# Raw DeltaNet tiles of the drain's sums in buffers of their own, inverses and turned outputs some steps later, in a hybrid mLSTM and DeltaNet layer

## The chip, the cores and the metric

The kernel runs on one core of a Trainium2 chip. The metric is the device time of one execution in microseconds; the median of several runs is given. Engine names are those of the profile: PE multiplies matrices, DVE, ACT and POOL do vector, activation and general work, SP issues transfers.

## What is computed

One layer of a decoder block on 512 tokens of width 2048, all in float32. A normalised input u is projected once; the parts feed an mLSTM with 8 heads and a gated DeltaNet with 16 heads; each branch's output goes through its half of the output projection, and the two results are gated and added to x, with a norm at the end.

```python
u = _rmsnorm(h, norm_w)
proj = jnp.matmul(u, w_in)                       # 2048 x 20528
h_a = _mlstm_chunkwise(q, k, v, i_pre, logf)     # 8 heads, chunks of 64
h_b = _gated_delta_chunkwise(dq, dk_, dv_, beta, g)
y_a = jnp.matmul(h_a, w_out[:ML_WIDTH])
y_b = jnp.matmul(h_b, w_out[ML_WIDTH:])
return jax.nn.sigmoid(gate_a) * y_a + jax.nn.sigmoid(gate_b) * y_b
```

In the DeltaNet each chunk solves a unit lower triangular system (the inverse below) before a chain over the chunks:

```python
a_mat = jnp.where(strict, bc[..., :, None] * kk * decay_mat, 0.0)
lhs = a_mat + jnp.eye(CHUNK)
sol = lax.linalg.triangular_solve(lhs, rhs, lower=True, unit_diagonal=True)
```

## The kernel before, in words

**Products.** Each float32 product is done as three matmuls: weights and activations are split into a high and a low part, and high·high, high·low and low·high are summed. A weight comes from memory into one of four buffers (`wr`, pool `wp`), ACT makes its high part (L135, `wh`) and DVE its low part (L138, `wl`). A list `plan` says in which order the weights are loaded (L176), and `prepare` keeps loads 4 and splits 3 weights ahead of PE.

**Stages by time in the trace.** Up to 100 us the input is prepared. To about 1060 the wide projections run as products of sums (seven matmuls in place of eight). From 1070 to 1846 the mixers run: eight units, each with two DeltaNet heads and, in four of them, one mLSTM head, whose projections (`proj_cm`, L250 to L265, bank `pj`) are interleaved with the mixers' small matmuls. From 1846 the output projection runs. Its mLSTM half is three wide blocks of 16 weights (`wide_block`, L1284 to L1286 in `products`): block 0 from 1846, block 1 from 1904, block 2 from 1966. Beside blocks 0 and 1 the last unit's inverse, back substitution and chain drain. From 2029 to 2187 the first part of the DeltaNet half runs as seven products (weights L505, their sums L528 and L535), and a last block ends at 2248.

**What sets the order.** PE's order is the program's. Side work is written as generators: `start(gen, wait)` puts one on a list, and `tick()`, called every six matmuls or so, lets each that is due issue its next piece; what it yields is the number of steps until the next. A step is some 1.4 us of matmuls. The instructions of the other engines are placed by a scheduler with priorities (`urgent`), and `behind(engine)` places one after the engine's newest weight split (for SP, its newest weight load). Each engine, and each engine's queue of transfers, then runs its instructions in that order.

**The parts that the change touches.**

- `turn` (L792) turns a finished output tile by a transpose on DVE (L796) into `to`, and `travel` (L799) issues four transfers of it on ACT's queue (L806) to h_d (DeltaNet) or hm_d (mLSTM) in memory, three steps after. For other tiles the same code issues on SP's queue, to `td` and back (L811).
- `dn_front_k` (L814) sends the DeltaNet's k products to memory and back in another layout, `ls` (L870), and inverts 128 systems of 32 by 31 pairs of DVE instructions (L881, L883). The result goes out and back (L895, L896) and is transposed into `tn` (L899), which the substitution reads (copies `ta` L951, `tb` L968; `vt` L972; matmuls `pw` L998). In the chain `r` (L993) and `st` (L1009) are DVE's, read by PE at L998 and L990.
- The conv rows: ACT copies a projection's bank out (`yp`, L770) and so frees the bank.
- `h_sums` (L1220) prepares the seven products. For each of eight pairs of DeltaNet heads it loads both heads' tiles of h_d (`hs`, `load_tile` L1177), makes three sums (L1237 to L1239) and a fourth in place (L1240) on DVE, stores that one to he_d from ACT's queue, and splits the sums (L1180, L1181). Its raw tiles come from `wp`, tag `wr`: the ring of four in which the weights lie. `load_h2` then loads the same h_d and he_d again as `hr` for the full products.
- `close` opens the pools for it: `sa2` when the first scratch pool (B) is no longer used, `sb2` when the second (A, `wk`) is free too. The last pair waits for `sb2`.
- The gates `tgy` of the wide blocks are loaded (L1299) into `wk` for block 0, tags `dm` and `rb`; block 1's into `wp`, tag `tg`.

Of the kernel before, what the change touches and what calls it, by code (L numbers as in the profile page):

```python
# [8 lines left out]
F32 = mybir.dt.float32  # L9
F32R = mybir.dt.float32r  # L10
AF = mybir.ActivationFunctionType
ALU = mybir.AluOpType
# [3 lines left out]
P = 128  # L16
S = 512
# [5 lines left out]
NO = 512  # L23
NRAW, NSPL = 4, 4
# [5 lines left out]
HP = S // 2  # L30
KH = KT // 2
# [15 lines left out]
UNITS = [(p, p + 1 if 2 * QKFIRST - 2 < p < 7 else None) for p in range(8)]  # L47
# [8 lines left out]
def hybrid_body(  # L56
# [16 lines left out]
    nc = tc.nc  # L73
    ctx.enter_context(tc.manual_schedule(engines={mybir.EngineType.PE}))
    V, A, G, T = nc.vector, nc.scalar, nc.gpsimd, nc.tensor
# [3 lines left out]
    wp = ctx.enter_context(tc.tile_pool(name="wp", bufs=4))  # L79
    dr = ctx.enter_context(tc.tile_pool(name="dr", bufs=1, space=DRAM))  # L80
    rows_d = dr.tile([32, S], F32, tag="rows", name="rows_d")
    h_d = dr.tile([KT, 16, BS, 4, BS], F32, tag="hd", name="h_d")
# [57 lines left out]
    def behind(eng):  # L140

        return tc.issue_after(newest[eng])
# [74 lines left out]
    def start(gen, wait=0, by=None):  # L217
        active.append([gen, clock["t"] + wait, held["by"] if by is None else by])
# [570 lines left out]
            with urgent():  # L789
                A.activation(jk, pk[:, c, :], AF.Square, accum_out=dst[:, c:c + 1])  # L790

    def turn(src, dst, out=False):  # L792


        o = dst if dst is not src and len(dst.shape) == 3 else wk.tile([P, NC, P], F32, tag="to", name="to", bufs=2)
        V.transpose(o if len(src.shape) == 3 else o.rearrange("p n c -> p (n c)"), src)  # L796
        start(travel(o, dst, out), 3 if out else 2)

    def travel(o, dst, out):  # L799

        d = dst if len(dst.shape) == 4 else dr.tile([16, BS, 4, BS], F32, tag="td", name="td", bufs=8)
        ov = o.rearrange("p n (j c) -> p (n j) c", c=BS)
        q = nc.scalar if out else nc.sync
        with behind("A") if out else urgent(2):
            for a in range(4):
                q.dma_start(d[:, :, a, :].rearrange("m r c -> r m c"), ov[a * BS:(a + 1) * BS])  # L806
        if d is dst:
            return
        yield 4
        with behind("A") if out else urgent(2):  # L810
            q.dma_start(dst, d.rearrange("(n j) r a c -> (j r) n (a c)", n=NC))  # L811
        yield 1

    def dn_front_k(hs, kq, u):  # L814
# [57 lines left out]
        G.memset(xi, 0.0)  # L872
        for q in range(4):
            G.memset(xi.rearrange("p m t -> p (m t)")[q * NSYS:(q + 1) * NSYS, q:(BS // 4) * BS:BS + 4], 1.0)
        yield 7
        for i in range(BS - 1):
            n, m = BS - 1 - i, i // 4 + 1
            tmp = wkb.tile([P, 80], F32, tag="tmp", name="tmp")
# [14 lines left out]
        with urgent():  # L893
            for q in range(4):
                nc.sync.dma_start(xd[:, :, :, q, :].rearrange("g b m t -> (g b) m t"), xi[q * NSYS:(q + 1) * NSYS])  # L895
            nc.sync.dma_start(tt, xd.rearrange("g b m q t -> (b m q) g t"))  # L896
        yield 14
        with urgent(), behind("V"):
            V.transpose(tn.rearrange("p g m -> p (g m)"), tt.rearrange("p g t -> p (g t)"))  # L899
        u.update(tn=tn, tt=tt)  # L900
# [75 lines left out]
    def dn_chain(j, hs, kq, u):  # L976
        h = hs[j]
        aq, qt, ke, ge = u["aq"][j], u["qt"][j], u["ke"][j], u["dm"][j][2]
        vn = u["vs"][j]

        po = pso.tile([P, NC, P], F32, tag="o", name="po")
        ssq = wk.tile([P, NC], F32, tag="ssq", name="ssq")
        st = None
        for c in range(NC):
            tsl = slice(c * P, (c + 1) * P)
            if st is None:
                r = vn[:, c, :]
            else:
                pr = psw.tile([P, P], F32, tag="wk", name="pr")
                T.matmul(pr, kq[j][:, 0, tsl], st, start=True, stop=True)  # L990
                r = wk.tile([P, P], F32, tag="r", name="r")
                with urgent():
                    V.scalar_tensor_tensor(out=r, in0=pr, scalar=negeg[:, c, h:h + 1], in1=vn[:, c, :],  # L993
                                           op0=ALU.mult, op1=ALU.add)
                T.matmul(po[:, c, :], qt[:, c, :], st, start=True, stop=False)
                yield 2
            pw = psw.tile([P, P], F32, tag="wk", name="pw")
            T.matmul(pw, tb[:, j * NC + c, :], r, start=True, stop=True)  # L998
            w = wk.tile([P, P], F32, tag="w", name="w")
            with urgent():  # L1000
                A.copy(w, pw)
            yield 2
            if c < NC - 1:
                pst = psw.tile([P, P], F32, tag="wk", name="pst")
                T.matmul(pst, ke[:, c, :], w, start=True, stop=True)
                sn = wk.tile([P, P], F32, tag="st", name="st", bufs=4)
                with urgent():
                    if st is None:
                        V.tensor_copy(sn, pst)  # L1009
                    else:  # L1010
                        V.scalar_tensor_tensor(out=sn, in0=st, scalar=ge[:, c:c + 1], in1=pst,
                                               op0=ALU.mult, op1=ALU.add)
            T.matmul(po[:, c, :], aq[:, c, 1, :], w, start=(st is None), stop=True)
            if c == 1:
                g = wk.tile([P, NC, P], F32, tag="g", name="gz", bufs=2)
                nc.sync.dma_start(g, gz_d[:, :, h * P:(h + 1) * P].rearrange("c p n -> p c n"))
            if c < NC - 1:
                st = sn
                yield 2

        jk = wk.tile([P, P], F32, tag="jk", name="jk", bufs=1)
        for c in range(NC):
            with urgent():
                A.activation(jk, po[:, c, :], AF.Square, accum_out=ssq[:, c:c + 1])
        with urgent():
            V.scalar_tensor_tensor(out=ssq, in0=ssq, scalar=1.0 / P, in1=u["qe"][:, j, :], op0=ALU.mult, op1=ALU.add)
        rsd = wk.tile([P, NC], F32, tag="rsd", name="rsd")
        G.tensor_tensor(out=rsd, in0=ssq, in1=mhalf, op=ALU.pow)
        G.tensor_tensor(out=g, in0=g, in1=bc(rsd, P), op=ALU.mult)
        yield 2  # L1030
        with urgent():
            V.tensor_tensor(out=g, in0=po, in1=g, op=ALU.mult)
        turn(g, h_d[h], True)

    def dn_unit(p, mh):
        hs = (2 * p, 2 * p + 1)
# [139 lines left out]
    def load_tile(dst, src):  # L1176
        nc.sync.dma_start(dst.rearrange("p (n t) -> p n t", n=NC), src.rearrange("(n j) r a c -> (j r) n (a c)", n=NC))  # L1177

    def split_scaled(hi, lo, src, w):
        A.activation(hi, src, AF.Copy, scale=w)  # L1180
        V.scalar_tensor_tensor(out=lo, in0=src, scalar=w, in1=hi.bitcast(F32), op0=ALU.mult, op1=ALU.subtract)  # L1181
# [35 lines left out]
    late = {}  # L1217
    he_d = dr.tile([KH, P, S], F32, tag="hed", name="he_d")

    def h_sums():  # L1220

        for i in range(KH):
            if i == KH - 1:
                while "sb" not in late:
                    yield 1
                yield 2
            su = (late["sa"] if i < KH - 1 else late["sb"]).tile([P, 2, 3, HP], F32R, tag=f"su{i}", name="tu", bufs=1)
            late["su"].append(su)
            raw = []
            for n in range(2):  # L1230
                raw.append(wp.tile([P, S], F32, tag="wr", name="hs", bufs=NRAW))
                load_tile(raw[n], h_d[2 * i + n])
            yield 3
            a11, a21, a12, a22 = (raw[n][:, m * HP:(m + 1) * HP] for n in range(2) for m in range(2))
            sf = late["sa"].tile([P, 3, HP], F32, tag="sf", name="hsum", bufs=2)
            with behind("V"):
                V.tensor_tensor(out=sf[:, 0], in0=a21, in1=a22, op=ALU.add)  # L1237
                V.tensor_tensor(out=sf[:, 1], in0=sf[:, 0], in1=a11, op=ALU.subtract)
                V.tensor_tensor(out=sf[:, 2], in0=a11, in1=a21, op=ALU.subtract)  # L1239
                V.tensor_tensor(out=a21, in0=a12, in1=sf[:, 1], op=ALU.subtract)  # L1240
            yield 1
            with behind("A"):
                nc.scalar.dma_start(he_d[i], raw[0])
            with behind("A"), behind("V"):
                split_scaled(su[:, 0], su[:, 1], sf, normc[:, 32:33])
            yield 3

    def load_h2():

# [21 lines left out]
    def close():  # L1271
        if "su" not in late and not using("B"):
            wkbs.close()
            sa = h2s.enter_context(tc.tile_pool(name="sa2", bufs=1, side="right"))
            late["sa"], late["su"] = sa, []
            start(h_sums(), 1)
        if "sb" not in late and "su" in late and not using("AB"):
            wks.close()
            sb = late["sb"] = h1s.enter_context(tc.tile_pool(name="sb2", bufs=1))
            late["X"] = sb.tile([P, 2, 2, NO], F32, tag="X", name="X2")  # L1280

    def products(ps, kt, c, hi, lo, ks):
        tsl = slice(c * P, (c + 1) * P)
# [7 lines left out]
    def wide_block(nb, pools, place, then=()):  # L1291
# [37 lines left out]
        for c in range(NC):  # L1329
# [6 lines left out]
            else:  # L1336
                start(put_last(), 1)

    DRAIN = (lambda c: wk.tile([P, NO], F32, tag=("dm", "rb")[c // 2], name="tgy", bufs=2 + c // 2),
             lambda c: wp.tile([P, NO], F32, tag="tg", name="tgy", bufs=3))  # L1340
    for b in range(YDRAIN):
        wide_block(b, ((psj, "pj"), (psw, "wk"), (psj, "pj"), (psj, "pj")), DRAIN[b])
# [281 lines left out]
```

## Time and profile before

| | |
|---|---|
| median of 3 runs | 2246.78 us (2246.72 to 2247.63) |
| profiled execution | 2249.86 us |
| its span, first to last instruction | 2247.8 us |
| PE busy | 2162.3 us (96%) |
| mean granted clock of TensorE | 0.990 |

The profiled execution is 3.1 us above the median; its span is 2.1 us below its own time. In the waits and groups a row reads: engine, output tile and line, what it waited for, then total us, times and the longest. In a timeline a row has start and duration in us, and in brackets how long the engine was idle before it and what released it. The granted clock is 1.00 at full speed and 0.50 at half.

### The profile page before, as it was taken

The numbers are of one execution on the slowest core, as the hardware profiler recorded it, in microseconds if no ns is written. First come the engines' busy times: TensorE is split into PE (matmuls) and PEld (weight loads), VectorE is DVE, ScalarE is ACT, GpSimd is POOL, SyncE is SP. The second block draws the span as 40 slices with busy tenths as digits, with TensorE's granted clock in tenths as the row PEclk, the third lists the DMA queues.
The fourth block names the chain that finished last, engine by engine and source line by source line (L and its number), as shares of the span: only waits on it lengthen the run. The fifth ranks groups of instructions, "written<-read, shape, count | busy, mean of one in ns | idle before, by whom it ended". The sixth has DMA issues, their size and how long they took to land. (4 is left out here: it accounts for less than half of the span.)

```text
span 2247.8 us, 31587 instructions
## 1 busy us (share of the span) xinstructions
PE 2162.3 (96%) x10592; PEld 1770.9 (79%) x10592; DVE 1671.8 (74%) x2907; ACT 995.1 (44%) x1890; POOL 280.7 (12%) x356
## 2 busy tenths in 40 slices
PE   7999999999999999999999999999999989879997
PEld 5878778888778888888878877888888877757775
DVE  5787788778877777876678877676767676557775
ACT  5444444445444443444444534444444443334344
POOL 0320000000000000000222422222222211100101
PEclk9999999999999999999999999999999999989999
DMA  5456666667666775776676866767665666595896
GB/s 156 128 171 198 198 195 214 206 191 234 203 214 223 230 233 179 229 253 193 171 187 164 198 150 147 174 167 183 168 162 145 169 170 176 149 271 172 242 327 213
DMA packets 534821, 435.81 MB, mean 194 GB/s; under 512 B 241921, under 2 KB 393698, under 8 KB 534530
## 3 DMA queue, kind: packets, MB, share of 16 engines
q1 hardware_dynamic: 425058, 357.68, 55.7%
q10 hardware_dynamic: 105568, 68.77, 9.7%
q0 software_dynamic: 4032, 7.34, 2.2%
q8 instruction: 83, 1.36, 0.3%
q14 instruction: 80, 0.66, 0.1%
HBM read 342.37 MB, written 95.49 MB: 195 GB/s over the span
## 5 line engine op out<-in xcount | busy, mean ns | idle before, releaser
L135 ACT CAST wh<-wr 128x512 fp32r<-128x512 f32 (+1 forms) x538 | 379.5, 707 | 477.3 <-PE pj L262 221.8
L138 DVE TENSOR_TENSOR wl<-wr,wh 128x512 fp32r<-128x512 f32 (+1 forms) x538 | 449.3, 838 | 168.3 <-ACT wh L135 159.5
L261 PE MATMUL pj<-uh,wh 128*128 128x512 f32 x1024 | 429.0, 419 | 3.1 <-ACT yp L770 3.1
L263 PE MATMUL pj<-uh,wl 128*128 128x512 f32 x1024 | 401.9, 393 | 0.0
L262 PE MATMUL pj<-ul,wh 128*128 128x512 f32 x1024 | 401.2, 392 | 0.0
L576 PE MATMUL ps<-wl,uh 128*128 128x512 f32 x704 | 277.3, 394 | 6.1 <-DVE wl L138 5.8
L575 PE MATMUL ps<-wh,uh 128*128 128x512 f32 x704 | 275.8, 392 | 3.7 <-DVE X L617 3.0
L577 PE MATMUL ps<-wh,ul 128*128 128x512 f32 x704 | 274.4, 390 | 0.0
L135 ACT CAST wh<-ts 128x512 fp32r<-128x512 f32 x224 | 138.1, 617 | 255.0 <-DVE ts L535 196.3
L135 ACT CAST wh<-t 128x1024 fp32r<-128x1024 f32 x112 | 117.8, 1052 | 258.4 <-PE ps L577 136.7
L263 PEld LDWEIGHTS pj<-uh,wl 128*128 128x128 f32 x1024 | 192.8, 188 | 42.6
L576 PE MATMUL ps<-wl,suh 128*128 128x512 f32 x576 | 224.3, 389 | 1.7 <-DVE wl L138 1.7
L575 PE MATMUL ps<-wh,suh 128*128 128x512 f32 x576 | 224.4, 390 | 0.8 <-ACT qk L353 0.4
L261 PEld LDWEIGHTS pj<-uh,wh 128*128 128x128 f32 x1024 | 193.8, 189 | 38.9 <-ACT yp L770 3.9
L577 PE MATMUL ps<-wh,sul 128*128 128x512 f32 x576 | 224.1, 389 | 0.0
L262 PEld LDWEIGHTS pj<-ul,wh 128*128 128x128 f32 x1024 | 193.9, 189 | 32.9
L138 DVE TENSOR_TENSOR wl<-ts,wh 128x512 fp32r<-128x512 f32 x224 | 153.8, 690 | 38.8 <-ACT wh L135 38.8
L138 DVE TENSOR_TENSOR wl<-t,wh 128x1024 fp32r<-128x1024 f32 x112 | 137.2, 1225 | 53.4 <-ACT wh L135 52.9
L576 PEld LDWEIGHTS ps<-wl,uh 128*128 128x128 f32 x704 | 132.1, 188 | 43.1 <-DVE wl L138 17.3
L575 PEld LDWEIGHTS ps<-wh,uh 128*128 128x128 f32 x704 | 132.1, 188 | 37.7 <-DVE X L617 10.2
L577 PEld LDWEIGHTS ps<-wh,ul 128*128 128x128 f32 x704 | 132.2, 188 | 26.6
L535 DVE TENSOR_TENSOR ts<-wr 128x512 f32<-128x512 f32 x112 | 77.3, 690 | 98.7 <-DMA wr<-t_d 74.4
(302 smaller groups left out, 3481.3 us busy)
## 6 DMA issues: line engine op xcount, KB each, us to landing
wr<-in_w_in_dram SPq DMA_DIRECT2D x704, 256.0 KB, 3.7
wr<-in_w_out_dram SPq DMA_DIRECT2D x138, 256.0 KB, 4.6
t_d<-ts ACTq DMA_DIRECT2D x96, 256.0 KB, 4.1
wr<-t_d SPq DMA_DIRECT2D x96, 256.0 KB, 4.0
wr<-in_w_in_dram SPq DMA_DIRECT2D x64, 128.0 KB, 3.4
xt<-in_x_dram SPq DMA_DIRECT2D x8, 512.0 KB, 7.2
tg_d<-X ACTq DMA_DIRECT2D x16, 256.0 KB, 6.1
tg_d<-to ACTq DMA_DIRECT2D x16, 256.0 KB, 5.5
```

Source lines behind the costliest of these rows:

```text
L135: newest["A"] = A.copy(hi, src).ins
L138: newest["V"] = V.tensor_tensor(out=lo, in0=src, in1=hi.bitcast(F32), op=ALU.subtract).ins
L261: T.matmul(ps[j], hi[:, k, wsl], uh[:, kt, :], start=(kt == 0), stop=False)
L262: T.matmul(ps[j], hi[:, k, wsl], ul[:, kt, :], start=False, stop=False)
L263: T.matmul(ps[j], lo[:, k, wsl], uh[:, kt, :], start=False, stop=(kt == KT - 1))
L535: V.tensor_tensor(out=ts[:, 0, :], in0=r[:, 0, :], in1=r[:, 2, :], op=ALU.subtract)
L575: T.matmul(ps[t], ah, hi, start=(g == "A" and i == 0), stop=False, skip_group_check=True)
L576: T.matmul(ps[t], ah, lo, start=False, stop=False, skip_group_check=True)
L577: T.matmul(ps[t], al, hi, start=False, stop=(i == KH - 1), skip_group_check=True)
```

## The change

1. Turned outputs (h_d, hm_d) are issued 5 steps after their transpose instead of 3, but for the last unit's two DeltaNet heads, which keep 3.
2. Each inverse begins 10 steps after its `ls` load instead of 7, and the transpose into `tn` comes 17 steps after the inverse's stores instead of 14.
3. The raw tiles of the sums leave the weights' ring. Even pairs lie in `ls` (the inverse's tile, one buffer), odd pairs in `rb` (three buffers, shared with a row broadcast and one gate tile), the last pair in `hs` of `sb2`. `h_raw` loads a pair ahead, behind SP's newest weight load; `h_pair` makes the sums. The sums now hold pool A, so that `sb2` opens after the seventh pair, and `h_last` does the eighth.
4. Of block 0's gates the fourth moves from `rb` to `wp`, tag `tg`.

```diff
-    def turn(src, dst, out=False):
+    def turn(src, dst, out=False, lag=5):
...
-        start(travel(o, dst, out), 3 if out else 2)
+        start(travel(o, dst, out), lag if out else 2)
...
-        yield 7
+        yield 10
         for i in range(BS - 1):
...
-        yield 14
+        yield 17
         with urgent(), behind("V"):
...
-        turn(g, h_d[h], True)
+        turn(g, h_d[h], True, 5 if h < 2 * UNITS[-1][0] else 3)
...
+    def h_raw(i):
+        if i == KH - 1:
+            raw = [late["sb"].tile([P, S], F32, tag="hs", name="hs", bufs=4) for _ in range(2)]
+        elif i % 2:
+            raw = [wk.tile([P, S], F32, tag="rb", name="hs", bufs=3) for _ in range(2)]
+        else:
+            pair = wk.tile([P, 2, S], F32, tag="ls", name="hs", bufs=1)
+            raw = [pair[:, n, :] for n in range(2)]
+        with behind("S"):
+            for n in range(2):
+                load_tile(raw[n], h_d[2 * i + n])
+        return raw
+
+    def h_pair(i, raw):
...
+        yield 2
+        with behind("A"):
+            nc.scalar.dma_start(he_d[i], raw[0])
+        with behind("A"), behind("V"):
+            split_scaled(su[:, 0], su[:, 1], sf, normc[:, 32:33])
+        yield 1
+
     def h_sums():
 
-        for i in range(KH):
-            if i == KH - 1:
-                while "sb" not in late:
-                    yield 1
-                yield 2
...
-            raw = []
-            for n in range(2):
-                raw.append(wp.tile([P, S], F32, tag="wr", name="hs", bufs=NRAW))
-                load_tile(raw[n], h_d[2 * i + n])
...
+        raws_ = [h_raw(0)]
+        yield 3
+        raws_.append(h_raw(1))
+        yield 4
+        for i in range(KH - 1):
+            yield from h_pair(i, raws_[i])
+            if i + 2 < KH - 1:
+                raws_.append(h_raw(i + 2))
             yield 3
+
+    def h_last():
+
+        yield 5
+        raw = h_raw(KH - 1)
+        yield 5
+        yield from h_pair(KH - 1, raw)
...
-            start(h_sums(), 1)
+            start(h_sums(), 1, "A")
...
+            start(h_last(), 1)
...
-    DRAIN = (lambda c: wk.tile([P, NO], F32, tag=("dm", "rb")[c // 2], name="tgy", bufs=2 + c // 2),
+    DRAIN = (lambda c: wk.tile([P, NO], F32, tag="dm", name="tgy", bufs=2) if c < 2 else
+             wk.tile([P, NO], F32, tag="rb", name="tgy", bufs=3) if c == 2 else wp.tile([P, NO], F32, tag="tg", name="tgy", bufs=3),
              lambda c: wp.tile([P, NO], F32, tag="tg", name="tgy", bufs=3))
```

PE's rows are the same 9634 in both kernels and in the same order. Lines from L1220 on shift by up to 23: the gates' load L1299 is L1321 in the changed kernel, the sums L1237 to L1240 are L1239 to L1242, the load of he_d L1259 is L1280.

**SP around block 2's first weights.** Loads of weights are L176, of raw tiles and heads L1177, of the seven products' weights L505. Before:

```order
L1299 DMA tgy<-tg_d 128x512
L176 DMA wr<-in_w_out_dram 128x512
L1177 DMA hs<-h_d 128x4x128
L505 DMA wr_19217<-in_w_out_dram 128x512 x3
L505 DMA wr_19243<-in_w_out_dram 128x512 x3
L505 DMA wr_19269<-in_w_out_dram 128x512 x3
L1259 DMA hr<-he_d 128x512
L1177 DMA hr<-h_d 128x4x128
L1259 DMA hr<-he_d 128x512
L1177 DMA hr<-h_d 128x4x128
L1177 DMA hs<-h_d 128x4x128
L176 DMA wr<-in_w_out_dram 128x512 x2
```

Now:

```order
L176 DMA wr<-in_w_out_dram 128x512 x4
L1321 DMA tgy<-tg_d 128x512
L176 DMA wr<-in_w_out_dram 128x512 x4
L505 DMA wr_19213<-in_w_out_dram 128x512 x2
L176 DMA wr<-in_w_out_dram 128x512
L505 DMA wr_19213<-in_w_out_dram 128x512
L505 DMA wr_19239<-in_w_out_dram 128x512 x3
L176 DMA wr<-in_w_out_dram 128x512
L505 DMA wr_19265<-in_w_out_dram 128x512 x3
L1280 DMA hr<-he_d 128x512
```

The weight's load behind the gate tile is the sixth of block 2 before; the next one stood behind the last pair's first tile, the nine L505 and five loads more. Now the four behind the gate tile are the seventh to the tenth, the last pair's tiles have gone further back, and the rest of the weights stand between the L505.

**DVE around the copy tb (L968) of the last unit.** The sums of a pair are L1237 to L1240 before and L1239 to L1242 now, their split L1181. Before:

```order
L1239 TENSOR_TENSOR hsum<-hs 128x256
L138 TENSOR_TENSOR wl<-wr,wh 128x512
L1237 TENSOR_TENSOR hsum<-hs 128x256
L1238 TENSOR_TENSOR hsum<-hsum,hs 128x256
L1240 TENSOR_TENSOR hs<-hs,hsum 128x256
L1181 SCALAR_TENSOR_TENSOR tu<-hsum,normc,tu 128x768
L138 TENSOR_TENSOR wl<-wr,wh 128x512
L972 TENSOR_TENSOR vt<-vt,nk 128x512 x2
L138 TENSOR_TENSOR wl<-wr,wh 128x512
L968 COPY tb<-p_18520 64x8x64
```

Now:

```order
L1239 TENSOR_TENSOR hsum<-hs 128x256
L1241 TENSOR_TENSOR hsum<-hs 128x256
L1240 TENSOR_TENSOR hsum<-hsum,hs 128x256
L138 TENSOR_TENSOR wl<-wr,wh 128x512
L972 TENSOR_TENSOR vt<-vt,nk 128x512 x2
L1242 TENSOR_TENSOR hs<-hs,hsum 128x256
L1181 SCALAR_TENSOR_TENSOR tu<-hsum,normc,tu 128x768
L138 TENSOR_TENSOR wl<-wr,wh 128x512
L968 COPY tb<-p_18506 64x8x64
```

The sums ahead of tb are the third pair's before and the second pair's now.

**ACT around the last unit's first bank copies (L770).** The h_d issues are two earlier heads' turned outputs. Before:

```order
L806 DMA h_d<-to 32x16x32
L135 CAST wh<-wr 128x512
L806 DMA h_d<-to 32x16x32 x2
L770 COPY yp_9097<-pj 128x512
L806 DMA h_d<-to 32x16x32
L771 ACTIVATE kq_16976<-yp_9097,convc 128x512
```

Now:

```order
L806 DMA h_d<-to 32x16x32 x3
L135 CAST wh<-wr 128x512
L806 DMA h_d<-to 32x16x32 x2
L770 COPY yp_9097<-pj 128x512
L806 DMA h_d<-to 32x16x32
L771 ACTIVATE kq_16975<-yp_9097,convc 128x512
```

Ahead of the copy stand three issues before and five now.

More of the change, by code (lines that the diff above doesn't have):

```diff
@@ L1218, in hybrid_body @@
     he_d = dr.tile([KH, P, S], F32, tag="hed", name="he_d")
-    def h_sums():
-        for i in range(KH):
-            if i == KH - 1:
-                while "sb" not in late:
-                    yield 1
-                yield 2
-            su = (late["sa"] if i < KH - 1 else late["sb"]).tile([P, 2, 3, HP], F32R, tag=f"su{i}", name="tu", bufs=1)
-            late["su"].append(su)
-            raw = []
-            for n in range(2):
-                raw.append(wp.tile([P, S], F32, tag="wr", name="hs", bufs=NRAW))
-                load_tile(raw[n], h_d[2 * i + n])
-            yield 3
[L1234 to L1246, printed above, removed]
@@ new lines, in h_pair @@
+    def h_pair(i, raw):
+        su = (late["sa"] if i < KH - 1 else late["sb"]).tile([P, 2, 3, HP], F32R, tag=f"su{i}", name="tu", bufs=1)
+        late["su"].append(su)
+        a11, a21, a12, a22 = (raw[n][:, m * HP:(m + 1) * HP] for n in range(2) for m in range(2))
+        sf = late["sa"].tile([P, 3, HP], F32, tag="sf", name="hsum", bufs=2)
+        with behind("V"):
+            V.tensor_tensor(out=sf[:, 0], in0=a21, in1=a22, op=ALU.add)
+            V.tensor_tensor(out=sf[:, 1], in0=sf[:, 0], in1=a11, op=ALU.subtract)
+            V.tensor_tensor(out=sf[:, 2], in0=a11, in1=a21, op=ALU.subtract)
+            V.tensor_tensor(out=a21, in0=a12, in1=sf[:, 1], op=ALU.subtract)
+        yield 2
[4 more added lines that the diff above has]
+        yield 1
```

## The prediction

> **What bounds the kernel now.** First the head of the page, then its busy times by stage.
>
> ```profile
> span 2247.8 us, 31587 instructions
> PE 2162.3 (96%) x10592; PEld 1770.9 (79%) x10592; DVE 1671.8 (74%) x2907; ACT 995.1 (44%) x1890; POOL 280.7 (12%) x356
> ```
>
> TensorE is busy 96% of the span, and the program order of its 9634 rows is the same in both kernels. So the change cannot alter TensorE's work, only its waits and the clock that it is granted. The question is which waits stand in the stages that the diff touches. The windows give PE's busy time, then PEld, DVE, ACT, POOL, the granted clock, the DMA share and GB/s.
>
> ```profile
> 1070.00:1826.00 756.00, 745.27 (x4291) 621.02 (x4291) 556.39 (x1352) 339.82 (x867) 201.85 (x252) 1.00 0.69 166
> 1840.00:1880.00 40.00, 35.07 (x150) 28.43 (x148) 31.75 (x75) 15.81 (x28) 5.79 (x5) 0.91 0.84 223
> 1880.00:1920.00 40.00, 33.11 (x237) 25.88 (x235) 20.78 (x50) 13.90 (x34) 6.05 (x10) 0.97 0.63 165
> 1960.00:2000.00 40.00, 25.60 (x107) 20.43 (x106) 22.42 (x34) 11.93 (x23) 6.71 (x7) 0.82 0.86 243
> 2029.00:2187.00 158.00, 154.52 (x670) 124.82 (x670) 122.26 (x158) 65.95 (x95) 11.03 (x13) 1.00 0.81 252
> ```
>
> The mixers lose 11 us in 756. The three rows of the drain and block 2 lose 26 us in 120 (40 - 35.07, 40 - 33.11, 40 - 25.60), and the clock is under 1 in each. What PE waited for there, with total us, times and longest:
>
> ```profile
> PE py L1284 <- ACT wh L135: 15.2, 2, 13.3
> PE pw L998 <- DVE tb L968: 5.9, 1, 5.9
> PE py L1284 <- ACT yp L770: 4.9, 2, 3.5
> PE py L1285 <- DVE wl L138: 1.6, 3, 1.1
> ```
>
> Single rows say where these are, and what a stall does to the clock. The columns are start, duration, what ran, and in brackets the idle time and its releaser.
>
> ```profile
> 1851.28 0.50 PE L1284 MATMUL py<-wh,uh 128*128 128x512 f32 x1 [3.51 <-ACT yp L770]
> 1853.67 0.80 PE L1284 MATMUL py<-wh,uh 128*128 128x512 f32 x1 [1.42 <-ACT yp L770]
> 1854.26 0.63 PE L1285 MATMUL py<-wl,uh 128*128 128x512 f32 x1
> 1854.69 0.63 PE L1286 MATMUL py<-wh,ul 128*128 128x512 f32 x1
> 1897.21 0.49 PE L1284 MATMUL py<-wh,uh 128*128 128x512 f32 x1 [1.87 <-ACT wh L135]
> 1921.11 0.79 PE L998 MATMUL pw<-vt,tb 128*128 128x128 f32 x2 [5.90 <-DVE tb L968]
> 1926.68 0.39 PE L1285 MATMUL py<-wl,uh 128*128 128x512 f32 x1
> 1926.91 0.39 PE L1286 MATMUL py<-wh,ul 128*128 128x512 f32 x1
> 1996.14 0.80 PE L1284 MATMUL py<-wh,uh 128*128 128x512 f32 x1 [13.28 <-ACT wh L135]
> ```
>
> I call the four places **A** (1851), **B** (1897), **C** (1921) and **D** (1996). Starts lie 0.23 us apart at 1926 and 0.43 at 1854: after a long stall TensorE runs at half speed. The windows of that state:
>
> ```profile
> 1852.80:1859.70 6.90, 6.03 (x14) 4.83 (x15) 6.52 (x14) 5.67 (x10) 0.00 (x0) 0.51 0.83 205
> 1917.70:1924.50 6.80, 3.39 (x10) 2.81 (x11) 3.36 (x6) 0.77 (x2) 0.00 (x0) 0.50 0.63 191
> 1986.00:2003.00 17.00, 5.75 (x13) 4.18 (x14) 14.53 (x20) 8.47 (x12) 0.86 (x1) 0.50 1.05 363
> ```
>
> Half of the busy time in such a window is lost: 3.0 us after A, 1.7 after C, 2.9 after D. So A costs 3.5 + 1.4 + 3.0 = 7.9 us, B 1.9, C 7.6, D 13.3 + 1.1 (the longest wait for wl, in the row above, is its second) + 2.9 = 17.3, together 34.7.
>
> [...]
>
> **The change part by part.**
>
> *D, the raw tiles leave the weights' ring.* The rows are SP's DMA issues; durations of an x9 row span all nine.
>
> ```profile
> 1971.10 1.09 SPq L176 DMA_DIRECT2D wr<-in_w_out_dram  x1
> 1978.29 0.38 SPq L1177 DMA_DIRECT2D hs<-h_d  x1
> 1979.94 4.21 SPq L505 DMA_DIRECT2D wr<-in_w_out_dram  x9
> 1989.18 1.68 SPq L176 DMA_DIRECT2D wr<-in_w_out_dram  x2
> ```
>
> Between two weights' loads of block 2 SP stood 18 us: first on the last pair's tile, which takes a buffer of the weights' ring and waited for the last heads' turned output in h_d, then in nine loads for the seven products (L505) and five of sums and heads. The weight issued at 1989.18 is the one that PE waits for at D. In the new order (front part, SP) no raw tile stands there, and ten of block 2's sixteen weights stand ahead of the first L505 instead of six. A weight gives PE 12 matmuls of 0.23 us, so 2.8 us; all four buffers of the ring are weights' again, and a load can go each 2.8 us as one frees. That removes D's cause. What is late next: the L505 loads and the sums' first DVE work (L528) now stand between the weights' low parts, and wait for loads that themselves come later. I see two such places, of 1 to 4 us each. I take 3 us left: **-14**, with bounds -17.3 (nothing left) and -9 (8 us left, clock included).
>
> *C, a pair ahead.* The rows are DVE's.
>
> ```profile
> 1909.77 0.43 DVE L1239 TENSOR_TENSOR hsum<-hs 128x256 f32<-128x256 f32 x1 [3.30 <-DMA hs<-h_d]
> 1915.15 0.43 DVE L1237 TENSOR_TENSOR hsum<-hs 128x256 f32<-128x256 f32 x1 [4.35 <-DMA hs<-h_d]
> 1920.38 0.68 DVE L968 COPY tb<-p 64x512 f32<-64x512 f32 x1
> ```
>
> DVE stood 3.30 and 4.35 us at the first sums of the third pair, whose raw tiles had not landed. Behind these in its order were the low parts of two weights, vt (L972) and tb, five microseconds of work from 1915.15 on, and PE waited for tb. In the new order only the first two pairs' sums stand ahead of tb, and their tiles are loaded ahead of the inverse's stores (L895); the third pair's sums stand behind tb. The 7.65 us of DVE's wait cover the 5.90 of PE's stall. **-7.6**, with bounds -7.6 and -3 (the second of the two waits, 4.35, still there).
>
> *B.* SP's queue, in 1830 to 2010, by what its next load waited for (total us, times, longest):
>
> ```profile
> SPq L176 <- DVE hsum L1237: 12.7, 5, 3.6
> SPq L176 <- DMA he_d<-hs: 7.4, 4, 4.1
> ```
>
> Weights' loads (L176) waited for the sums and their stores, because these held the ring's buffers; the load behind B is one of the five. With buffers of their own a weight's load waits for a low part alone. **-1.9**, bounds -1.9 and 0.
>
> *A, outputs 2 steps later.* ACT's rows:
>
> ```profile
> 1846.21 0.40 ACTq L806 DMA_DIRECT2D h_d<-to  x1
> 1848.52 2.08 ACTq L806 DMA_DIRECT2D h_d<-to  x2
> 1850.65 0.58 ACT L770 COPY yp<-pj 128x512 f32<-128x512 f32 x1 [3.31 <-DMA vt<-td]
> ```
>
> The copy L770 that empties a projection's bank stands behind DMA issues of turned outputs, which wait for earlier transfers. Two steps of lag change which stand there: in the new order five issues are ahead of the first L770 instead of three, and one behind it as before (front part, ACT). Each goes when an earlier transfer has landed, and those transfers keep their place beside PE's work, so the last of the five should go about when the last of the three did. I take **0**: bounds -7.9 (all of A) and +2.1 (two more issues at the 1.04 us of the x2 row).
>
> *Inverses 3 steps later, in the mixers.* DVE issues in order, and L881 needs ls, which has gone out to memory and back.
>
> ```profile
> 1299.37 0.19 DVE L881 TENSOR_TENSOR tmp<-ls,xi 128x31 f32<-128x31 f32 x1 [4.90 <-DMA ls<-ld]
> 1300.77 0.49 PE L998 MATMUL pw<-r,tb 128*128 128x128 f32 x2 [2.26 <-DVE r L993]
> 1389.64 0.19 DVE L881 TENSOR_TENSOR tmp<-ls,xi 128x31 f32<-128x31 f32 x1 [5.85 <-DMA ls<-ld]
> 1390.15 0.49 PE L990 MATMUL pr<-st,kq 128*128 128x128 f32 x2 [2.02 <-DVE st L1009]
> ```
>
> At 1300 the later start puts r (L993) ahead of L881: -2.3. At 1390 the order is worse: L881 now stands ahead of both copies of st instead of one, so the 5.85 us wait can cover both: between -2 and +4.5 (2.4 more, and a half clock of some 2, as C's 1.7), and I take +1.5. The turning of tn at L899 moves with its reader. Sum **-1**, bounds -4 and +4.
>
> *Behind the drain.* Loads of the next seven products keep their order but get some 20 us less of stall to run ahead in. The bytes of 1960 to 2187 stay, 243 and 252 GB/s in the windows above against 363 at 1986; 20 us less makes about 275. **+1**, bounds 0 and +4.
>
> [...]
>
> Sum: -14 - 7.6 - 1.9 + 0 - 1 + 1 = **-23.5**. The profiled execution took 2249.86 us, its span 2247.8, and the runs' median is 2246.78, 3.1 less: so 2226.4 for an execution like the profiled one, and **2223** for the median.
>
> **Rivals.**
>
> 1. *A new wait in block 2 takes half of D.* The L505 loads and L528 stand between weights, and ACT's and DVE's queues are in order. For it: a DMA share of 1.05 in D's window. Against it: the ten weights ahead. Gain of D 6 instead of 14: **2231**.
> 2. *A goes*, if the issues' transfers land two steps sooner than I read: -7.9 more, **2215**.
> 3. *Slower: SP's head waits for shared buffers.* Raw tiles now share "ls" (one buffer) and "rb" (three, with the gates' tiles). A raw load waits for the store of an earlier sum (he_d) or of an output (y_d), and every weight stands behind it in SP's queue. How long a weight's load takes, in 1965 to 1996 (KB each, median us to landing):
>
> ```profile
> wr<-in_w_out_dram SPq DMA_DIRECT2D x12, 256.0 KB, 5.6
> ```
>
> With four buffers of 2.8 us a load is issued up to 11 us early and takes 5.6 to land, so SP can be held 5.4 us before PE starves; the longest wait behind a he_d store in the rows under B is 4.1. It decides from holds of 11.3 us: then each of the five later pairs costs C's 5.9, and 5 x 5.9 - 23.5 = +6 gives **2253**. Against it: the order gives each raw load a whole pair's time, and the wait of 4.1 is far from 11.3.
>
> 4. *It does nothing measurable*, because the scheduler places loads by buffers alone and PE is held to the same transfers: **2247**. The orders differ exactly at C and D, which speaks against it.
>
> **Chances.** Forecast, 2216 to 2230: 0.55. Rival 1, to 2241: 0.20. Rival 2 and better, to 2208: 0.12. Rival 3: 0.07. Rival 4: 0.06. A measurement of this kernel can tell about 0.2%, 4.5 us, from no change. Faster by more: 0.55 + 0.20 + 0.12 = 0.87; within: 0.06; slower: 0.07. The range leaves out rivals 3 and 4. Its low end is all terms at their better bounds, -17.3 - 7.6 - 1.9 - 7.9 - 4 + 0 = -38.7, so 2208; its high end is the four unsure ones, D, C, the mixers and what lies behind, at their worse bounds at once, -9 - 3 - 1.9 + 0 + 4 + 4 = -5.9, so 2241.
>
> **What will show it.** C and B: no idle of PE over 1 us on tb L968 and none on wh in blocks 0 and 1. D: the longest wait of py for wh in block 2 under 4 us, and the clock of that stretch above 0.95. A: the two yp waits about where they are. Mixers: the r wait of 2.3 gone, st's at 1390 as large or larger. Wrong would be a PE wait of over 5 us on wh behind a raw tile's load (rival 3), or the same 13 us at D (rival 4).

## The result, and the profile after

The changed kernel takes **2235.1 us** (median of 5 runs, 2233.9 to 2240.6) against 2246.7 (5 runs): ratio **0.9955**, 95% interval 0.9941 to 0.9970. That is 10 us less by the ratio (11.6 by the medians), and not the 23.5 of the sum. Its profiled execution took 2233.9 us, the shortest of the five, with a span of 2232.1; so the traces differ by 15.7 us, somewhat more than the medians. All medians and ratios here are of executions at the usual speed; one of e6's four took 7678 us and is in neither.

The windows of the changed kernel's trace, in the columns of before:

```profile
1070.00:1826.00 756.00, 739.29 (x4230) 616.12 (x4229) 547.29 (x1340) 334.39 (x855) 192.44 (x249) 0.99 0.68 165
1840.00:1880.00 40.00, 37.72 (x176) 30.91 (x175) 35.84 (x81) 22.50 (x51) 6.46 (x6) 1.00 0.86 225
1880.00:1920.00 40.00, 40.00 (x273) 32.48 (x272) 26.88 (x68) 15.27 (x38) 7.45 (x11) 1.00 0.88 229
1960.00:2000.00 40.00, 38.11 (x167) 30.87 (x166) 27.26 (x42) 15.79 (x25) 3.84 (x5) 1.00 1.02 296
```

The three rows of the drain hold 115.8 us of PE's work in 120, where they held 93.8, and their clock is 1.00. The row of the mixers has lost 6 us of PE's busy time (739.29 for 745.27), and some of its clock (0.99 for 1.00): the work that it should hold in 756 us now ends later. What PE waits for in 1820 to 2020, as total us, times and longest:

```profile
PE py L1306 <- ACT yp L770: 2.3, 2, 1.7
PE py L1307 <- DVE wl L138: 2.3, 3, 1.3
PE py L1306 <- ACT wh L135: 2.0, 1, 2.0
PE ps L575 <- DVE X L1329: 0.9, 1, 0.9
```

The wait for tb (5.9) and that of 13.3 us for wh are not there. In the mixers, from 1060 to 1826:

```profile
PE p L966 <- ACT s L962: 7.8, 4, 2.6
PE pj L261 <- ACT yp L770: 4.2, 3, 2.1
PE pr L990 <- DVE st L1009: 2.4, 1, 2.4
PE pw L998 <- DVE tb L968: 1.4, 1, 1.4
```

The first row was 0.7 us, once, before. It stands in four units, one row of the timeline each (start, duration, idle time):

```profile
1466.07 0.33 PE L966 MATMUL p<-tb,s 64*64 64x64 f32 x2 [2.59 <-ACT s L962]
1578.01 0.38 PE L966 MATMUL p<-tb,s 64*64 64x64 f32 x3 [1.67 <-ACT s L962]
1687.88 0.32 PE L966 MATMUL p<-tb,s 64*64 64x64 f32 x2 [1.25 <-ACT s L962]
1800.39 0.32 PE L966 MATMUL p<-tb,s 64*64 64x64 f32 x2 [2.25 <-ACT s L962]
```

And this is ACT ahead of the first of them, in the changed kernel:

```profile
1460.87 0.62 ACT L135 CAST wh<-wr 128x512 fp32r<-128x512 f32 x1
1463.13 0.93 ACTq L806 DMA_DIRECT2D hm_d<-to  x2
1464.18 0.62 ACT L135 CAST wh<-wr 128x512 fp32r<-128x512 f32 x1 [2.69 <-PE pj L263]
1465.01 0.31 ACTq L806 DMA_DIRECT2D hm_d<-to  x1
1465.42 0.59 ACT L962 ACTIVATE s<-p 64x512 f32<-64x512 f32 x1 [0.63 <-DMA wr<-in_w_in_dram]
```

The same place in the kernel before:

```profile
1455.64 5.10 ACTq L806 DMA_DIRECT2D hm_d<-to  x4
1460.78 0.74 ACT L955 COPY tb<-p 32x256 f32<-32x256 f32 x2 [4.60 <-DMA hm_d<-to]
1461.54 1.14 ACT L135 CAST wh<-wr 128x512 fp32r<-128x512 f32 x2
1462.71 0.59 ACT L962 ACTIVATE s<-p 64x512 f32<-64x512 f32 x1
```

Nothing on ACT is busy for long; in the changed kernel its queue stands at issues of the mLSTM heads' turned outputs (hm_d), which in the kernel before have all gone ahead of L955. The idle time of 2.69 us is put down to PE, by a matmul of L263 that ended at 1463.48. In the kernel before, the second L135 ran right behind the first, before the matmul in the same place had begun (1462.24), so it does not need that one. What held the queue was the row ahead, whose two issues could not go before 1463.13. Six of this head's eight issues went 0.02 to 0.10 us after an earlier transfer had landed, the one at 1465.01 after a weight's load that landed at 1464.99.

PE's rows are the same in both kernels, so the same matmul can be found in both traces. Its start, and how much later (+) or earlier (-) the changed kernel has it:

| PE's matmul | before | after | difference | what lies between |
|---|---|---|---|---|
| first conv row of a projection, L261 | 1138.26 | 1138.60 | +0.3 | |
| a projection of the last mLSTM unit, L262 | 1793.33 | 1805.35 | +12.0 | mixers **+11.7** |
| last unit's chain, L998 | 1830.63 | 1841.06 | +10.4 | -1.6 |
| block 0, L1284 | 1858.95 | 1864.26 | +5.3 | A **-5.1** |
| block 0, L1285 | 1897.94 | 1900.34 | +2.4 | B **-2.9** |
| the last unit's chain, L998 | 1924.47 | 1919.05 | -5.4 | C **-7.8** |
| block 2, L1284 | 2002.90 | 1979.96 | -22.9 | D -17.5 |
| block 2, L1284 | 2022.90 | 2004.35 | -18.6 | D given back +4.4 |
| last block, L1284 | 2193.53 | 2178.23 | -15.3 | behind +3.3 |

The drain gave what was forecast, and more at A. The mixers took 10 us back. From 1400 to 1793 of the kernel before they lose 11.2 us; the four waits are 7.8, and half of the three stretches of half clock that follow them (last section) is 5.1; e1, which has none of them, wins 1.5 in the same stretch.

### The profile page after: what moved, and what is told of

Same layout as the page of the kernel before. It is cut to its first block, busy times and chain, and to the rows that moved or that the text cites. A ratio compares the mean times of both kernels' runs of the same rounds, so it can differ in the third digit from the quotient of the medians.

```text
span 2232.1 us, 31548 instructions
## 1 busy us (share of the span) xinstructions
PE 2159.3 (97%) x10592; PEld 1771.9 (79%) x10592; DVE 1671.0 (75%) x2907; ACT 995.0 (45%) x1890; POOL 276.6 (12%) x356
## 5 line engine op out<-in xcount | busy, mean ns | idle before, releaser
L135 ACT CAST wh<-wr 128x512 fp32r<-128x512 f32 (+1 forms) x538 | 379.9, 707 | 470.9 <-PE pj L262 261.8
L261 PE MATMUL pj<-uh,wh 128*128 128x512 f32 x1024 | 431.6, 421 | 4.2 <-ACT yp L770 4.2
L263 PE MATMUL pj<-uh,wl 128*128 128x512 f32 x1024 | 404.3, 395 | 0.0
L262 PE MATMUL pj<-ul,wh 128*128 128x512 f32 x1024 | 403.2, 394 | 0.0
L135 ACT CAST wh<-ts 128x512 fp32r<-128x512 f32 x224 | 138.2, 617 | 256.3 <-DVE ts L535 192.2
L135 ACT CAST wh<-t 128x1024 fp32r<-128x1024 f32 x112 | 117.9, 1053 | 250.9 <-PE ps L577 122.8
L263 PEld LDWEIGHTS pj<-uh,wl 128*128 128x128 f32 x1024 | 194.1, 190 | 43.3
L261 PEld LDWEIGHTS pj<-uh,wh 128*128 128x128 f32 x1024 | 195.2, 191 | 40.8 <-ACT yp L770 5.4
L262 PEld LDWEIGHTS pj<-ul,wh 128*128 128x128 f32 x1024 | 195.6, 191 | 33.4
L577 PEld LDWEIGHTS ps<-wh,ul 128*128 128x128 f32 x704 | 132.5, 188 | 26.7
```

Of the source, the lines that this page charges most:

```text
L135: newest["A"] = A.copy(hi, src).ins
L261: T.matmul(ps[j], hi[:, k, wsl], uh[:, kt, :], start=(kt == 0), stop=False)
L262: T.matmul(ps[j], hi[:, k, wsl], ul[:, kt, :], start=False, stop=False)
L263: T.matmul(ps[j], lo[:, k, wsl], uh[:, kt, :], start=False, stop=(kt == KT - 1))
L577: T.matmul(ps[t], al, hi, start=False, stop=(i == KH - 1), skip_group_check=True)
```

## The experiments

All ratios are to the kernel before, run on the same chip with it; 1% is 22.5 us.

| label | what it is | median us | ratio (95% interval) |
|---|---|---|---|
| (the change) | buffers, inverses later, outputs later | 2235.1 | 0.9955 (0.9941 to 0.9970) |
| e1_lag3 | buffers, inverses later | 2216.6 | 0.9867 (0.9847 to 0.9887) |
| e2_yields | buffers, outputs later | 2244.3 | 0.9984 (0.9970 to 0.9998) |
| e3_lag_alone | outputs later | 2264.8 | 1.0079 (1.0057 to 1.0100) |
| e4_buffers_alone | buffers | 2237.3 | 0.9945 (0.9925 to 0.9966) |
| e12_inverses_alone | inverses later | 2227.8 | 0.9902 (0.9885 to 0.9918) |
| e5_lag_dn_only | as the change, mLSTM outputs at 3 | 2220.8 | 0.9888 (0.9869 to 0.9907) |
| e6_begin_late_alone | as e1, read at the old 14 | 2220.8 | 0.9894 (0.9871 to 0.9917) |
| e7_read_late_alone | as e1, begun at the old 7 | 2227.8 | 0.9914 (0.9890 to 0.9937) |
| e8_begin_13 | as e1, begun at 13, read at 14 | 2213.3 | 0.9846 (0.9822 to 0.9869) |
| e9_lag7 | as the change, mLSTM outputs at 7 | 2238.7 | 0.9958 (0.9945 to 0.9972) |
| e10_lag10 | as the change, mLSTM outputs at 10 | 2228.0 | 0.9915 (0.9882 to 0.9949) |
| e11_begin13_lead22 | as e8, block 2's lead at 22 | 2216.6 | 0.9862 (0.9836 to 0.9888) |

**The parts, one taken out and one alone.** Theory 1: the later issue of hm_d makes the new waits at L962. Theory 2, the rival: the later inverses move the substitution, and L962 with it.

```diff
# e1: the changed kernel, outputs at 3 again
-    def turn(src, dst, out=False, lag=5):
+    def turn(src, dst, out=False, lag=3):
...
-        turn(g, h_d[h], True, 5 if h < 2 * UNITS[-1][0] else 3)
+        turn(g, h_d[h], True, 3)
```

> The changed kernel with turned outputs issued 3 steps later again. Theory 1 (the later issues of hm_d stand in ACT's queue between the copies L955 and the activation L962 of four mixer units, four of them each, and PE waits for L962): the four waits p <- s L962 (7.8 us) and the half clocks behind them go, some 10 to 12 us, so 2223 to 2226 (the changed kernel 2235), unless the lag is also what shortened the two waits for L770 at the start of block 0, then 5 us less of it, 2229. Theory 2 (the inverses' later start moves the substitution, and so L962): 2235 as the changed kernel.

Measured 2216.6, below every value expected. The four waits at L962 are gone; in 1060 to 1830 PE waits for

```profile
PE pj L261 <- ACT yp L770: 1.9, 1, 1.9
PE pw L998 <- DVE r L993: 1.7, 1, 1.7
PE p L966 <- ACT s L962: 1.4, 1, 1.4
PE pk L841 <- DVE kq L780: 1.1, 2, 0.7
```

The remaining L962 is in another unit, at 1280, where two issues of hm_d stand ahead of it in the kernel before too. And the two waits for L770 at block 0 are as short as with the lag (1.4 and 0.8 us), so the lag had not shortened them. Theory 1 stands; the lag costs 0.0088 of the time, some 20 us.

```diff
# e2: the changed kernel, inverses at the old steps
-        yield 10
+        yield 7
...
-        yield 17
+        yield 14
```

> The changed kernel with the inverses begun and read at the old steps (7 and 14). Theory 1: the four waits for L962 stay; the wait for r at 1300 us (2.3) comes back and that for st near 1387 shrinks, so 2235 within 3. Theory 2: the four waits go, 2224.

Measured 2244.3. The waits at L962 stay in three of the four units (1.0, 2.1 and 1.5 us), so theory 2 falls. But the time is 9 us above the changed kernel's (6.5 by the ratios), more than theory 1 allowed: the later inverses gain something that neither theory had. Block 0's waits for L770 are 3.6 and 0.8 us here.

```diff
# e3: the kernel before, with part 1 of the change alone
...
-        start(travel(o, dst, out), 3 if out else 2)
+        start(travel(o, dst, out), lag if out else 2)
...
```

> The kernel before with the later issue of turned outputs alone. Theory 1: the four waits for L962 appear, +10 to +12, and the start of block 0 loses at most 5, so 2252 to 2258. Theory 2: 2247 as before.

Measured 2264.8, ratio 1.0079: slower by 18 us, the waits at L962 in all four units (1.8, 1.7, 2.7 and 0.3 us), and nothing won at block 0 (3.6 and 1.0 us). The lag harms by itself.

```diff
# e4: the changed kernel, outputs at 3, inverses at 7 and 14
-    def turn(src, dst, out=False, lag=5):
+    def turn(src, dst, out=False, lag=3):
...
-        yield 10
+        yield 7
...
-        yield 17
+        yield 14
...
```

> The kernel before with the sums' buffers and the pair loaded ahead alone (inverses and outputs as before). Theory 1: the gains at tb, at the weight of block 0 and in block 2 stay (24 us less some 3 given back behind), the mixers are as before, so 2224 to 2228. Theory 2: the same within 2. If the drain's gain needs the later inverses or the lag, 2235 or more.

Measured 2237.3: the buffers alone win 12 us, half of the 24 expected. The long waits at C and D are gone, but the one at A has stayed (4.9 before) and others have come, in 1826 to 2015:

```profile
PE py L1306 <- ACT yp L770: 5.5, 2, 4.0
PE py L1306 <- ACT wh L135: 4.5, 2, 4.0
PE py L1307 <- DVE wl L138: 2.1, 2, 1.7
```

Beside the kernel before, the matmul of block 2 that started at 2002.48 there is 22.5 us earlier, 26.7 gained since block 0 began; by the start of the seven products 9.6 of that are lost again, among them 4.0 at the last weight of block 2.

**What the later inverses win.**

```diff
# e12: the kernel before, with part 2 of the change alone
-        yield 7
+        yield 10
...
-        yield 14
+        yield 17
```

> The kernel before with the inverses begun at 10 and read at 17 steps, alone. If their gain in the mixers (some 17 us of 2237 to 2217, with the sums' buffers changed) does not hang on the buffers: 2227 to 2233, with waits of PE for L881's followers (st, r, c) gone between 1138 and 1400 us and the two waits for L770 at block 0 halved, while the waits of the drain (tb 5.9, wh 13) stay. If it was a difference of chips or needs the buffers: 2243 to 2250.

Measured 2227.8, as the first branch expected: 22 us from two numbers. PE's rows, compared as in the table above, tell where. The figures are what each stretch is longer (+) or shorter (-) by than in the kernel before, whose times bound the stretches:

| run | up to 1060 | mixers, to 1831 | drain and blocks 0 to 2, to 2023 | behind |
|---|---|---|---|---|
| (the change) | +0.8 | +9.6 | -29.0 | +2.9 |
| e1, buffers and inverses | -1.8 | -8.2 | -26.1 | +5.4 |
| e2, buffers and outputs | -0.3 | +10.7 | -21.9 | +4.3 |
| e3, outputs | +6.1 | +12.0 | -1.8 | +1.0 |
| e4, buffers | -1.2 | +4.9 | -18.8 | +5.1 |
| e12, inverses | -0.9 | -8.0 | -13.8 | +1.5 |

No edit touches what runs up to 1060, and e4's touches nothing in the mixers; there the traces still differ by up to 6.1 and 4.9 us, and differences of that size in one trace can be chance. So some 8 of e12's 22 us come in the mixers (e1 has as many), and 14 in the drain, which the buffers shorten too.

In the mixers, 1060 to 1830, PE's waits fall by 4.5 us in all (10.7 to 6.2). DVE's fall by more. Of the kernel before, from 1100 to 1880:

```profile
DVE tmp L881 <- DMA ls<-ld: 23.3, 8, 5.9
DVE tn L899 <- DMA tt<-xd: 19.5, 5, 5.2
```

Of e12, the same stretch; there is no row for L899:

```profile
DVE tmp L881 <- DMA ls<-ld: 9.8, 3, 4.9
```

DVE stood 43 us at the head of its queue for two transfers, and now stands 10. With all that, the drain's waits were no longer what they were; e12 in 1826 to 2015:

```profile
PE py L1284 <- ACT wh L135: 9.5, 2, 8.9
PE py L1285 <- DVE wl L138: 3.0, 3, 2.5
PE py L1284 <- ACT yp L770: 2.8, 2, 2.2
PE pw L998 <- DVE tb L968: 1.1, 1, 1.1
```

The wait for tb is 1.1 instead of 5.9 and the one at B is gone, though the raw tiles are still in the weights' ring. So C and B had two cures, D only the buffers (net it is 1.1 us shorter here), and A (4.9 to 2.8) hangs on the inverses, not on the lag. One of the expectation's details was wrong: the drain's waits did not stay.

```diff
# e6: e1, read at 14
-        yield 17
+        yield 14
# e7: e1, begun at 7
-        yield 10
+        yield 7
```

> The kernel with 3 steps of lag, inverses begun 10 steps after their load, but read at 14 (3 steps sooner than with 17). If the gain of the later inverses (2237 to 2217) is DVE no longer standing at L881 for ls: 2217 within 3. If it is the later transpose into tn: 2235.

> The kernel with 3 steps of lag, inverses begun at 7 steps, but read at 17. The opposite: 2235 if the begin makes the gain, 2217 if the transpose does.

Neither branch was right: each of the two wins about half, 0.9894 and 0.9914 between 0.9945 with none and 0.9867 with both. DVE's waits at the two lines fall in both, but not in step with the time. For e6:

```profile
DVE tmp L881 <- DMA ls<-ld: 7.0, 2, 4.6
DVE tn L899 <- DMA tt<-xd: 3.4, 1, 3.4
```

For e7:

```profile
DVE tmp L881 <- DMA ls<-ld: 18.9, 7, 4.8
DVE tn L899 <- DMA tt<-xd: 1.5, 1, 1.5
```

With the old steps (e4) they are 45 us, with the later begin alone 10, no more than with both (12 in e1), and with the later reading alone 20. So it is likely, but not shown, that the mixers' gain is DVE's time at these two lines.

```diff
# e8: e1, begun at 13, read at 14
-        yield 10
+        yield 13
...
-        yield 17
+        yield 14
```

> As with 3 steps of lag, inverses begun 13 steps after their load and read at 14, the same sum of 27 as 10 and 17. If the begin is what counts and ls still lands late at 1297 us (PE waited 1.7 us for r there): some 2 to 4 us less than 2217. If the later begin pushes the inverse's own end into the substitution: 2220 or more, with waits of PE on tn or tb.

Measured 2213.3, 0.9846: 3 us below e1, at the edge of what these runs can tell (the intervals overlap). The wait for r is 0.4 us instead of 1.7. It is the best version that was run.

**Which outputs, and why.**

```diff
# e5: the changed kernel, mLSTM outputs at 3
-    def turn(src, dst, out=False, lag=5):
+    def turn(src, dst, out=False, lag=3):
```

> The changed kernel with the DeltaNet heads' outputs 5 steps late and the mLSTM heads' 3 steps. If all of the lag's 18 us hang on the mLSTM outputs (hm_d) in front of L962: 2217, as with 3 steps everywhere. If the DeltaNet heads' outputs carry the part of it that is not at L962 (the waits at 1138, 1252, 1284, 1387 us, some 7 us in the traces): 2224.

Measured 2220.8, 0.9888, between the two values; its interval and that of e1 overlap. The waits at L962 in the four units are gone with the mLSTM heads' lag alone. In the trace two waits of 2.3 and 2.1 us appear at 1255 and 1286 that e1 has not (1.4 at the second), so the DeltaNet outputs may carry some 4 us; this is not settled.

```diff
# e9 (7) and e10 (10): the changed kernel; the DeltaNet heads' outputs name their own lag
-    def turn(src, dst, out=False, lag=5):
+    def turn(src, dst, out=False, lag=7):
```

> The changed kernel with outputs 7 steps late (the last unit's two heads keep 3). In ACT's order the four units then have 5, 5, 5 and 6 issues of hm_d between L955 and L962, instead of 4 each. If it is this place in the queue that costs: at least the changed kernel's waits for L962 (7.8 us in four), 2235 to 2240.

> The changed kernel with outputs 10 steps late: all issues of the four units then stand behind L962, none between L955 and it. If the place in the queue costs: the four waits for L962 are gone and the time is 2217 to 2224, as with 3 steps, although the outputs go out later than in the changed kernel. If lateness itself costs (tiles held longer, stores that land later): 2235 or more.

Both edits move the mLSTM outputs alone; the DeltaNet outputs stay at 5 steps, as in e5. The run with 3 steps to compare with is therefore e5. e9 came as expected. e10 lies above the 2217 to 2224 expected for the queue, and 7 us above e5, but the intervals of these two overlap. With 7 steps, from 1400 to 1826:

```profile
PE p L966 <- ACT s L962: 11.9, 4, 4.1
```

With 10:

```profile
PE pst L1005 <- ACT w L1001: 5.5, 3, 2.5
```

At 10 steps the issues have passed L962 and stand ahead of the chain's w (L1001): the wait has moved to what is behind them, and is shorter. The time goes 2221, 2235, 2239, 2228 with the mLSTM outputs at 3, 5, 7 and 10 steps; the cost follows the place in ACT's queue, not the lateness alone.

**Block 2's remainder.**

```diff
# e11: e8, the seven products' lead later
-    wide_block(YDRAIN, banks[1], lambda c: X2[:, c // 2, c % 2, :], [(load_h2(), 1), (lead(), 18)])
+    wide_block(YDRAIN, banks[1], lambda c: X2[:, c // 2, c % 2, :], [(load_h2(), 1), (lead(), 22)])
```

> The kernel with 3 steps of lag and inverses begun at 13 and read at 14 steps, and the seven products' first loads and sums begun 22 steps into block 2 instead of 18. If the waits of block 2 that came in place of the 13 us (PE for wl near 1962 and 1972, for wh near 1983) hang on the first sums (L528) standing between weights' low parts: 4 to 8 us less than with 18, 2206 to 2210 beside 2213. If the loads are what is late there: no less, with longer waits at the first of the seven products (ps).

Measured 2216.6, not less than e8. The wait at the last weight falls from 2.3 us to none, but a wait of 1.7 us comes at the first of the seven products and the two for wl stay. What delays these stays open.

## Why the prediction went wrong, point by point

- **D.** Right: -17.5 and 4.4 given back, net -13.1 against -14. With the buffers alone (e4) it is -8.7. The two places in block 2 were there, as waits of 0.6 and 1.3 us for wl and one of 2.0 for wh; DVE stood 6.8 us for the first sums (L528).
- **C** and **B.** Right: -7.8 against -7.6, and -2.9 against -1.9; the buffers alone give -7.8 and -2.8 (e4). That both would have shrunk with the inverses alone (e12) was not seen: the gain was attributed to the buffers.
- **A.** The forecast was 0; it fell by 5.1, some 3 of it the half clock that no longer follows (0.51 in the prediction's window behind A, 1.00 from 1840 to 1880 now), and the sign named for A (the two waits about where they are) did not hold: 4.9 became 2.3. The five issues ahead of L770 were read as the lag's, but they come with the inverses' later begin. Five stand there in e1, e6 and e12, with 3 steps of lag, and three in e2 and e3, with 5. The waits follow: 2.1, 2.2 and 2.8 us in the first three, 4.4 and 4.6 in the other two.
- **Behind the drain.** +3.3 against +1, within its bounds.
- **Outputs 2 steps later: the step that failed.** "Two steps of lag change which stand there" was followed at block 0 only, and costed at 0. The edit moves the outputs of every head. In the four units with an mLSTM head of their own it put four issues of hm_d between L955 and L962, which PE waits for; at block 0 it changed neither ACT's order nor the time (e3: -0.2 us). e1, e3, e5, e9 and e10 show that this costs: 18 us by itself (e3), 20 with the rest (e1). The order of ACT around L962 would have told it: in these four units none stand there in the kernel before.
- **Inverses 3 steps later: the second that failed, the other way.** "Sum -1, bounds -4 and +4" came from the two PE waits that named L881's followers, and stood for the mixers alone. By itself (e12) the edit wins some 8 us in the mixers and 14 in the drain, where the prediction gave it no term. In the changed kernel, beside the lag, the mixers' part does not show (+9.6, and +10.7 without it in e2); the drain's does (-29.0, and -21.9 without it). The places were searched by PE's waits, whose releasers are r, st, c or yp; the waits of DVE itself, 43 us at two lines, are one row each and were not read.

The two errors have opposite signs: without the lag the change gives 30 us, more than the 23.5 forecast; with it 10. The prediction had no rival for a wait in the mixers other than the one at 1390 (2.0 before, 2.4 after). The time lies where rival 1 put it, 2231 to 2241, but not for its reason: D did not lose half of its gain.

The parts do not add up: alone they are -12, -22 and +18 us, together -10 rather than -16. The larger part of this is that buffers and inverses cure the same waits of the drain: -18.8 and -13.8 alone, -26.1 together (e1).

## What to carry to other kernels

An edit to a helper is costed at every call of it, and on the queue that its transfers are issued from: list what stands behind each of them there. And an engine that is not the bottleneck is read by its own waits too: where DVE stood at the head of its queue for a transfer here (4.90 us at L881 for ls, at 1299 in the kernel before), r behind it was late, and PE's wait of 2.26 us named r, not the transfer. The steps of delay, with which DVE stood 10 us at such waits instead of 43, won more by themselves than the buffers: 22 us (e12) against 12 (e4). Where a gain arises is told by the same PE rows in both traces, stage by stage; the total alone would have put all of e12's 22 us into the mixers.

## What the runs showed of the hardware

The half clock came after stalls much shorter than C's (5.90 us) or A's (3.51), but not after each. Windows of the changed kernel behind the four waits at L962 (the clock is the third figure from the end):

```profile
1467.63:1471.04 3.41, 3.41 (x10) 2.66 (x9) 3.38 (x6) 1.47 (x3) 0.00 (x0) 0.50 0.74 198
1578.50:1581.90 3.40, 3.40 (x24) 2.87 (x22) 2.92 (x5) 2.51 (x5) 0.64 (x1) 1.00 0.87 231
1689.49:1692.90 3.41, 3.41 (x9) 2.63 (x8) 3.38 (x5) 1.41 (x3) 0.77 (x1) 0.50 0.77 195
1802.13:1805.54 3.41, 3.41 (x10) 2.66 (x9) 3.38 (x6) 1.29 (x3) 0.00 (x0) 0.50 0.45 131
```

A stall of 1.25 us was followed by it, one of 1.67 was not. The three stretches of half clock in these windows begin at distances that are whole multiples of 3.413 us (1467.63 to 1689.49 is 65 of them, to 1802.13 is 98), and each lasts 3.41; in the kernel before, the one behind A lasts 6.83, C's 6.83 and D's 17.07, two, two and five times as long. The gaps of 1.25, 2.25 and 2.59 us were followed by one stretch each, 1.7 us of PE's time (half of 3.41). The length of a gap does not decide it alone: 1.87 us at B in the kernel before and 1.98 at 2004 in the changed kernel, both with matmuls of 128x512 on either side, were followed by none. Behind each of the four gaps at L962 come 1.1 us of matmuls of 64x64 (16 of them). Whether these small matmuls or the moment at which a gap falls made the difference, no run here separates. Among the changed kernel's five runs the shortest (2233.9 us) had a mean clock of 0.994 and the longest (2240.6) one of 0.990; the three between do not keep the order.
